# Late modulation in bursts of two k-tiles, and a smaller spacing of the recurrence's level pairs, in a hybrid decoder step

## Chip, cores and metric

The kernel runs on one core of one Trainium2 chip. The metric is the device time of one execution in microseconds (us); the span is the time from the first to the last instruction of the profiled execution.

## The reference

One decoder layer is applied to a prompt of 512 tokens and to 8 x 4 sample tokens with a cached past; both lie side by side as 544 token columns. All of it is fp32.

- A conditioning vector per sequence (9 in all) gives six modulation vectors: `mod = silu(c) @ w_ada + b_ada`, split into `sh1, sc1, g1, sh2, sc2, g2`.
- `h = rmsnorm(x) * (1 + sc1) + sh1`, and `proj = h @ w_in` is split into the queries, keys and values of an attention (8 heads of 64), the inputs of a gated linear recurrence (4 heads of 128) and two gates.
- The attention is block-sparse; for the sample tokens it reads 2048 cached rows per sequence through a page table.
- The recurrence is `S_t = diag(f_t) S_{t-1} + k_t v_t^T, o_t = S_t^T q_t`, followed by an rmsnorm over its 128 features and a gate.
- `mixed = sigmoid(ga) * (o_a @ w_a) + sigmoid(gb) * (o_b @ w_b)`, `x += g1 * (mixed @ w_o)`.
- A second modulated rmsnorm with `sc2, sh2`, a gated feed-forward with a causal convolution (`w_up`, `w_down`), `x += g2 * ...`, and a final rmsnorm.

`g1`, `sh2`, `sc2` and `g2` are not needed before `w_o`; they are the late modulation.

## The kernel before

Features stand on the 128 partitions, tokens along the free axis, in two halves of 272 columns. Every large product `W @ X` is made of three matmuls in fp32r (high part by high part, high by low, low by high). A weight chunk of four 128 x 128 tiles is loaded by SP's queue (`weights`, L206), rounded by ScalarE (`whi`), subtracted by VectorE (`wlo`), and used for twelve matmuls on each half of the tokens. So half a chunk, twelve matmuls, is the unit in which the main work advances (`pieces`, L296).

The order of TensorE's instructions is the order in which the program writes them, from the pool of the projections to `finish_sides` in L1262 (a manual schedule for TensorE alone; the other engines' order is made by the framework). It is set by a planner in the kernel itself. `Paced` (L101) keeps a clock of its own: each matmul adds `(0.006 + n * ns) * cols / 128` us, with n moving columns and ns 0.00044 for fp32r and 0.00167 for fp32, and 0.095 us are added when the shape of the array tile changes. The main work is a generator, `run_jobs` (L1125), which takes projection jobs in the order `ORDER` and then the products with `w_a` (`last_jobs`, L1252). Beside it run side generators; each yields how many us from now it is due again, and whether its next step is tiled, which means that it works on 32 columns of the array. After each half chunk `weave` calls `serve` (L273):

```
            if flat:
                run(flat[0])
            elif due and (len(due) > 1 or pe.t - due[0].due > due[0].slack or pe.mode[1] < 128):
                run(due[0])
```

A step that is not tiled runs when it is due. A tiled step runs when another is due too, when it is over `SLACK` = 2.5 late, or when the array is in a narrow mode already. The tiled sides here are these:

- `moba` (L708), the cached attention: 16 sets of scores and 16 of values, one every `SETS` = 7.2.
- `recur` (L1037), the recurrence on the prompt: per head four pairs of levels (64 and 32, 16 and 8, 4 and 2, 1 and 0), each pair a burst of 32-column matmuls (`level_mm`), then `yield LV, True`. After a head's last pair, `rec_gather` makes `rec_out` due 6.5 later, and the next head's decay work makes `rec_turn` due 8.0 after its first pair was prepared; both are full-width.
- `ada_late` (L1150), the late modulation, calls `ada_rest` (L1074) for two slabs of `w_ada`. Each has eight k-tiles of 128 x 2048 (1 MB). The tile `wadl` has two buffers, and its loads are issued by ScalarE's queue. The four quarters of the array each take 512 columns of a k-tile with the 32 padded conditioning columns `cs`; they accumulate in one PSUM bank over the eight k-tiles. The slab's result is copied into another buffer of the same tag, transposed and added to the bias.

`recur_sample` (L1164) is the recurrence on the sample tokens, two heads at a time; it starts a pair of heads when their `ob` is there, and has two tiled steps in it (the state products `QEs`), due 6.0 and 5.0 after the step before. It ends with the norm: for each head a square on ScalarE and a matmul with a matrix of 1/128. `ada_late` and `recur_sample` become sides when both attentions are done and the job then running is finished. After the main work, `finish_sides` runs what is left. Then the recurrence's output is scaled, split into `obh` and `obl`, and multiplied by `w_b`, then `w_o`, `w_up`, `w_down`.

Of the kernel before, what the change touches and what calls it, by code (L numbers as in the profile page):

```python
# [9 lines left out]
F32 = mybir.dt.float32  # L10
# [38 lines left out]
LNEXP = "natural_log_exp_and_others"  # L49
NPG = 9  # L50
WR, WS = 4, 3
SLACK, LT, SETS, LV, ADA = 2.5, 3.0, 7.2, 7.0, 3.6
ORDER = "k0 v0 k1 k2 k3 v1 v2 v3 f0 q0 i0 f1 q1 i1 f2 q2 i2 f3 q3 i3 a0 a1 a2 a3 a4 a5 a6 a7 g0 g1 g2 g3"
LATE = ("a4", "a5", "a6", "a7")
LAST = "b0 b1 b2 b3 b4 b5 b6 b7"
# [83 lines left out]
def layer_kernel(ctx, tc, i, o):  # L139
    nc = tc.nc  # L140
    sync, act, dve, pool, pe = nc.sync, nc.scalar, nc.vector, nc.gpsimd, Paced(nc.tensor)
# [11 lines left out]
    def gbank():  # L153
        return bank("g", NG)
# [10 lines left out]
    def mbank():  # L165
        return bank("macc", 1)
# [30 lines left out]
    def tt(out, a, b, op):  # L197
        return dve.tensor_tensor(out, a, b, op=op)  # L198
# [140 lines left out]
    cs = pC.tile([128, 8, 32], F32, name="cs")  # L339
# [733 lines left out]

    def ada_rest(sl, v0):  # L1074
        pa = mbank()
        for k in range(8):
            w = pT_.tile([128, 4, 512], F32, name="wadl", tag="wadl", bufs=2)
            act.dma_start(w, i["w_adl"][sl, k])
            yield ADA, True
            for g in range(4):  # L1080
                pe.matmul(pa[32 * g:32 * g + 32, :], cs[:, k, :], w[:, g, :], start=k == 0, stop=k == 7,
                          skip_group_check=True)
        sm = pT_.tile([128, 512], F32, name="smr", tag="wadl", bufs=2)
        dve.tensor_copy(sm, pa)
        yield 4.0
        pt = gbank()
        for c in range(4):
            pe.transpose(pt[:, 128 * c:128 * c + 128], sm[:, 128 * c:128 * c + 128], ident)
        pv = pt.rearrange("p (c g r) -> p c g r", c=4, g=4)
        for c in range(4):  # L1090
            for v in range(2):
                tt(modT[:, v0 + v, slice(c, 8, 4), :], pv[:, c, 2 * v:2 * v + 2, :9],
                   bada[:, v0 + v, slice(c, 8, 4), None].to_broadcast([128, 2, 9]), OP.add)
# [45 lines left out]
    pT_ = tc.alloc_tile_pool(name="rec", bufs=1, reuse_waits="tile")  # L1139
# [10 lines left out]
    def ada_late():  # L1150
        yield from ada_rest(0, 2)
        yield from ada_rest(1, 4)
        dve.scalar_tensor_tensor(modT[:, 4], modT[:, 4], 1.0, n2g[:, :, None].to_broadcast([128, 8, 9]),
                                 op0=OP.add, op1=OP.mult)
# [378 lines left out]
```

## Time and profile before

| | us |
|---|---|
| median of 3 runs | 979.36 |
| lowest and highest run | 977.35, 980.24 |
| profiled execution, its time | 979.07 |
| its span | 977.4 |
| TensorE busy in the span | 945.6 |

The profiled execution is 0.29 us below the median. A row of the timeline gives start and duration in us from the span's start; matmuls are pipelined, so a duration is longer than the distance to the next start. An fp32 matmul of the program shows as two records, so one modulation k-tile is eight records. In the stretches, the clock is the granted share of TensorE's full speed.

### The profile page before, as it was taken

How to read it: one execution, taken by the hardware profiler on the slowest of the kernel's cores; microseconds unless marked ns; L12 is line 12 of the kernel's file. 1: busy time of each engine (PE TensorE's matmuls, PEld its weight loads, DVE VectorE, ACT ScalarE, POOL GpSimd, SP SyncE). 2: the span in 40 equal slices, each digit the busy share in tenths (PEclk: the TensorE clock that was granted, in tenths of full speed). 3: DMA queues.
4: the chain of work that ended last, by engine and by line, in shares of the span. 5: the costliest groups of instructions: out<-in, count | busy, mean ns of one | idle time of the engine just before them, and what ended most of it. 6: DMA issues, size and time to landing. Idle time of an engine off the chain costs nothing.

```text
span 977.4 us, 23999 instructions
## 1 busy us (share of the span) xinstructions
PE 945.6 (97%) x8951; PEld 870.8 (89%) x8951; DVE 579.4 (59%) x1488; ACT 471.7 (48%) x942; POOL 103.1 (11%) x164
## 2 busy tenths in 40 slices
PE   5999999999999999999999999999999999999994
PEld 3898888877779988889998999999999999999994
DVE  5654546454657868755886676655555555555553
ACT  4344645543554645232544466544444444555452
POOL 1221222212210000000042200000000000001011
PEclk9999999999999999999999999999999999999997
DMA  9799999989695465473246143222222223566661
GB/s 361 283 363 374 360 332 341 332 289 340 237 358 186 165 209 183 161 276 119 65 147 212 45 130 126 99 90 87 87 87 88 87 90 92 175 178 188 196 175 67
DMA packets 89430, 190.06 MB, mean 194 GB/s; under 512 B 10337, under 2 KB 17634, under 8 KB 87266
## 3 DMA queue, kind: packets, MB, share of 16 engines
q1 hardware_dynamic: 75826, 140.74, 42.5%
q0 software_dynamic: 8160, 26.75, 7.6%
q10 hardware_dynamic: 5328, 21.05, 6.1%
q8 instruction: 70, 1.15, 0.5%
q14 instruction: 46, 0.38, 0.1%
HBM read 181.47 MB, written 7.02 MB: 193 GB/s over the span
## 4 chain that ended last, share of the span: by engine, by line
PE 74%; DVE 2%; ACT 1%; issue 1%; DMA 1%; POOL 0%; DVEq 0%; ACTq 0%; POOLq 0%
PE g L123 64%; PE macc L123 4%; PE s L123 2%; PE acc L123 1%; DMA wraw<-in_w_o 1%; PE s L127 1%; DVE wlo L198 1%; PE g L127 0%; POOL tgb L1281 0%; DVE hl L1283 0%; PE ms L123 0%; DVE tgb L1279 0%; ACT hh L195 0%; DVE tga L1461 0%; DVE wol L198 0%
## 5 line engine op out<-in xcount | busy, mean ns | idle before, releaser
L198 DVE TENSOR_TENSOR wlo<-wraw,whi 128x512 fp32r<-128x512 f32 (+1 forms) x300 | 203.2, 679 | 208.3 <-ACT whi L195 204.3
L195 ACT ACTIVATE whi<-wraw 128x512 fp32r<-128x512 f32 (+1 forms) x300 | 185.5, 619 | 258.2 <-PE g L123 237.3
L123 PE MATMUL g<-hh,whi 128*128 128x272 f32 x712 | 212.2, 299 | 1.3 <-ACT hh L195 1.0
L123 PE MATMUL g<-hl,whi 128*128 128x272 f32 x712 | 205.4, 289 | 0.7 <-DVE hl L1283 0.7
L123 PE MATMUL g<-hh,wlo 128*128 128x272 f32 x712 | 205.4, 288 | 0.6 <-DVE wlo L477 0.5
L123 PE MATMUL g<-h2h,whi 128*128 128x272 f32 x704 | 202.3, 289 | 0.0
L123 PE MATMUL g<-h2l,whi 128*128 128x272 f32 x704 | 201.3, 287 | 0.0
L123 PE MATMUL g<-h2h,wlo 128*128 128x272 f32 x704 | 198.8, 288 | 0.0
L123 PEld LDWEIGHTS g<-hh,whi 128*128 128x128 f32 x712 | 134.1, 188 | 16.7 <-issue 11.8
L123 PEld LDWEIGHTS g<-hl,whi 128*128 128x128 f32 x712 | 134.3, 189 | 1.3 <-DVE hl L1283 0.9
L123 PEld LDWEIGHTS g<-hh,wlo 128*128 128x128 f32 x712 | 134.0, 188 | 1.0 <-DVE wlo L477 0.7
L123 PEld LDWEIGHTS g<-h2l,whi 128*128 128x128 f32 x704 | 132.4, 188 | 0.1
L123 PEld LDWEIGHTS g<-h2h,whi 128*128 128x128 f32 x704 | 132.3, 188 | 0.2
L123 PEld LDWEIGHTS g<-h2h,wlo 128*128 128x128 f32 x704 | 130.8, 188 | 0.0
L123 PE MATMUL g<-ah,wlo 128*128 128x272 f32 x352 | 101.3, 288 | 1.2 <-DVE wlo L198 1.2
L123 PE MATMUL g<-ah,whi 128*128 128x272 f32 x352 | 101.8, 289 | 0.0
L123 PE MATMUL g<-al,whi 128*128 128x272 f32 x352 | 101.5, 288 | 0.0
L123 PEld LDWEIGHTS g<-ah,wlo 128*128 128x128 f32 x352 | 66.1, 188 | 1.5 <-DVE wlo L198 1.4
L123 PEld LDWEIGHTS g<-ah,whi 128*128 128x128 f32 x352 | 66.3, 188 | 0.1
L123 PEld LDWEIGHTS g<-al,whi 128*128 128x128 f32 x352 | 66.2, 188 | 0.1
L1323 POOL TENSOR_TENSOR sq<-sq,sq 128x272 f32<-128x272 f32 x24 | 20.9, 872 | 385.9 <-ACT sq L1314 374.1
L1417 DVE SCALAR_TENSOR_TENSOR cv<-U,sv,cv 128x560 f32<-128x560 f32 x44 | 35.3, 802 | 16.5 <-ACT cv L1415 15.7
(313 smaller groups left out, 1480.5 us busy)
## 6 DMA issues: line engine op xcount, KB each, us to landing
wraw<-in_w_up SPq DMA_DIRECT2D x98, 256.0 KB, 2.5
wraw<-in_w_in SPq DMA_DIRECT2D x82, 256.0 KB, 4.5
wraw<-in_w_down SPq DMA_DIRECT2D x80, 256.0 KB, 2.9
pg<-in_K SPq DMA_DIRECT2D x77, 256.0 KB, 6.7
pg<-in_V SPq DMA_DIRECT2D x77, 256.0 KB, 6.8
wadl<-in_w_adl ACTq DMA_DIRECT2D x16, 1024.0 KB, 5.8
pg<-in_K POOLq DMA_DIRECT2D x51, 256.0 KB, 6.0
pg<-in_V POOLq DMA_DIRECT2D x51, 256.0 KB, 6.2
```

What stands on the lines that cost most here:

```text
L123: return self.eng.matmul(out, lhsT, rhs, **kw)
L127: return self.eng.transpose(out, in_, ident)
L195: return act.activation(out, in_, AF.Copy, scale=scale)
L198: return dve.tensor_tensor(out, a, b, op=op)
L1323: pool.tensor_tensor(sqa[f], sqa[f], s, op=OP.add)
L1417: dve.scalar_tensor_tensor(a, U[:, t:t + W], cw[:, t, j:j + 1], a, op0=OP.mult, op1=OP.add)
```

## The change

The late modulation takes two k-tiles at a time: both loads are issued, 7.2 us later both are due, and their eight matmuls are issued together. Before, it was one load, 3.6 us, four matmuls. The number of buffers of `wadl` stays at two. `LV`, the time after which the recurrence's next pair of levels is due, goes from 7.0 to 6.0.

```diff
-SLACK, LT, SETS, LV, ADA = 2.5, 3.0, 7.2, 7.0, 3.6
+SLACK, LT, SETS, LV, ADA = 2.5, 3.0, 7.2, 6.0, 3.6
...
     def ada_rest(sl, v0):
         pa = mbank()
-        for k in range(8):
-            w = pT_.tile([128, 4, 512], F32, name="wadl", tag="wadl", bufs=2)
-            act.dma_start(w, i["w_adl"][sl, k])
-            yield ADA, True
-            for g in range(4):
-                pe.matmul(pa[32 * g:32 * g + 32, :], cs[:, k, :], w[:, g, :], start=k == 0, stop=k == 7,
-                          skip_group_check=True)
+        for k0 in range(0, 8, 2):
+            ws = [pT_.tile([128, 4, 512], F32, name="wadl", tag="wadl", bufs=2) for _ in range(2)]
+            for w, k in zip(ws, (k0, k0 + 1)):
+                act.dma_start(w, i["w_adl"][sl, k])
+            yield 7.2, True
+            for w, k in zip(ws, (k0, k0 + 1)):
+                for g in range(4):
+                    pe.matmul(pa[32 * g:32 * g + 32, :], cs[:, k, :], w[:, g, :], start=k == 0, stop=k == 7,
+                              skip_group_check=True)
         sm = pT_.tile([128, 512], F32, name="smr", tag="wadl", bufs=2)
```

## Rows read from the trace of the kernel before

**Rows 1.** The page, busy time, share of the span and instructions of each engine.

```profile
PE 945.6 (97%) x8951; PEld 870.8 (89%) x8951; DVE 579.4 (59%) x1488; ACT 471.7 (48%) x942; POOL 103.1 (11%) x164
```

**Rows 2.** Stretches: length, busy us (instructions) of each engine, clock, DMA share, GB/s.

```profile
480.00:488.00 8.00, 7.57 (x56) 6.95 (x56) 6.72 (x14) 2.47 (x4) 0.52 (x1) 1.00 0.25 66
517.00:521.50 4.50, 2.74 (x16) 1.92 (x15) 2.82 (x13) 3.16 (x6) 0.12 (x1) 1.00 0.48 176
521.50:525.50 4.00, 3.79 (x18) 3.74 (x18) 3.64 (x8) 2.32 (x5) 1.93 (x2) 0.57 0.44 146
```

**Rows 3.** TensorE's timeline around one burst: start, duration, what ran.

```profile
321.56 0.29 PE L123 MATMUL g<-hl,whi 128*128 128x272 f32 x1
321.69 0.29 PE L123 MATMUL g<-hh,wlo 128*128 128x272 f32 x1
321.91 1.07 PE L123 MATMUL macc<-wadl,cs 128*32 128x512 f32 x8
322.79 0.78 PE L123 MATMUL s<-EX 128*32 128x32 f32 x64
323.50 0.39 PE L123 MATMUL g<-hh,whi 128*128 128x272 f32 x1
323.73 0.29 PE L123 MATMUL g<-hl,whi 128*128 128x272 f32 x1
```

**Rows 4.** TensorE's timeline, three other bursts with modulation matmuls.

```profile
329.71 1.07 PE L123 MATMUL macc<-wadl,cs 128*32 128x512 f32 x8
...
345.43 1.06 PE L123 MATMUL macc<-wadl,cs 128*32 128x512 f32 x8
...
429.97 1.06 PE L123 MATMUL macc<-wadl,cs 128*32 128x512 f32 x8
```

**Rows 5.** The tile wadl: its matmuls (ns min/median/max, first and last start), time to landing.

```profile
L123 PE MATMUL macc<-wadl,cs x128: 592/593/618, 321.9 to 441.2; 128*32 128x512 f32 x128
...
DMA to landing us min/median/max: 4.7/5.8/8.9
```

**Rows 6.** TensorE's timeline in the cached attention: sets (macc), pairs of levels (EX).

```profile
282.62 0.76 PE L123 MATMUL s<-EX 128*32 128x32 f32 x64
...
291.27 1.92 PE L123 MATMUL macc<-pg,pT 128*32 128x512 f32 x16
...
299.98 1.92 PE L123 MATMUL macc<-pg,pT 128*32 128x512 f32 x16
...
302.57 0.51 PE L123 MATMUL s<-EX 128*32 128x32 f32 x33
```

**Rows 7.** TensorE's timeline at the end of the recurrence.

```profile
413.27 0.48 PE L123 MATMUL s<-EX 128*32 128x32 f32 x32
...
420.66 0.61 PE L123 MATMUL acc<-hs,V 128*128 128x128 f32 x4
...
434.17 0.62 PE L123 MATMUL acc<-s,QEs 128*32 128x512 f32 x2
...
441.60 1.03 PE L123 MATMUL acc<-s,QEs 128*32 128x512 f32 x4
...
454.12 0.63 PE L123 MATMUL s<-rv,kvx 96*128 96x512 f32 x2
...
471.38 1.08 PE L123 MATMUL s<-EX,con 128*128 128x272 f32 x4
...
482.64 0.39 PE L123 MATMUL g<-obh,whi 128*128 128x272 f32 x1 [0.40 <-ACT obh L195]
```

**Rows 8.** VectorE's timeline between the norm matmuls and the splits.

```profile
473.66 0.43 DVE L1242 TENSOR_SCALAR rr<-s 128x272 f32<-128x272 f32 x1
...
483.82 1.37 DVE L198 TENSOR_TENSOR obl<-ob,obh 128x544 fp32r<-128x544 f32 x2
```

**Rows 9.** ScalarE's timeline between the norm matmuls and the splits.

```profile
474.18 1.12 ACT L1246 ACTIVATE rr<-rr 128x1088 f32<-128x1088 f32 x1 [1.73 <-issue]
...
475.93 1.10 ACT L1248 ACTIVATE rr<-rr 128x1088 f32<-128x1088 f32 x1
```

## The prediction

> **What bounds the kernel now.** I read the page's engine table first: TensorE is busy for 945.6 of 977.4 us [rows 1], so between the start and the last stage only two things can change the time: what TensorE has to do, and whether it is ever left without work. The changed lines act between about 280 and 480 us. I therefore read TensorE's timeline there, burst by burst, and then the join at 481 us, where the last `w_a` matmul is followed by the first `w_b` matmul, which needs the normalised recurrence output.
>
> A burst in which the array works on quarters of 32 columns looks like [rows 3]: full-width matmuls start at 321.56 and 321.69 (0.125 apart, before rounding), the burst at 321.91, a modulation k-tile takes 0.88, a pair of levels 0.71, and after it the second full-width matmul comes 0.23 after the first. So going in costs 0.22 - 0.125 = 0.095 us and coming out about 0.1: some 0.2 per burst.
>
> The join has no slack. The last of the four norm matmuls of the recurrence starts at 471.38 [rows 7]; from it a chain of VectorE and ScalarE work leads to the split `obh`/`obl`, whose last piece is written from 483.82 on for 1.37 us (two instructions) [rows 8], and TensorE waits 0.40 us for `obh` at 482.64 [rows 7]. In the 8 us around it TensorE is idle for 8.00 - 7.57 = 0.43 us [rows 2]. So an earlier recurrence gains at most about 0.4 us here; a later one is paid for almost in full. When the recurrence ends is set by the planner, so the change has to be followed through it.
>
> **The change, part by part.**
> *Work on TensorE.* Nothing is added or removed: 128 records of modulation matmuls before [rows 5], eight for each of 16 k-tiles, and the same after. What may go is mode switches. Of the 16 k-tiles only two stand in a burst with no other narrow work beside them, at 345.43 and 429.97 [rows 4]; the others share their burst with a pair of levels or with another 32-column step. Two bursts less are 2 x 0.2 = **-0.4 us**.
> The Trainium skill, TensorEngine Tiling (Array Packing), Key Properties, says that a change of tiling mode drains TensorE; read alone, 16 bursts made into 8 would spare 8 such round trips. By that the sum would be 8 x 0.2 = -1.6 us instead of -0.4.
>
> *The pace.* The planner's clock, from the code: half a chunk (12 matmuls) 1.508, a k-tile 0.861, a pair of levels 0.345 to 0.505, a switch 0.095. Tiled steps run when two are due, or when one is 2.5 late.
> Before: a burst at T with the k-tile first makes it due again at T+4.56 and the pair at T+8.43. The planner looks at T+3.04, 4.54, 6.05, 7.56. At 7.56 the k-tile is over 2.5 late and goes, and at its end the pair is due too. Period 7.56; measured 329.71 - 321.91 = 7.80 [rows 3, 4], so a burst takes 0.24 more than planned.
> After: pair at T, then two k-tiles. The pair is due at T+6.57, the modulation at T+9.49. At 8.42 the pair alone is 1.85 late, which is allowed; at 9.93 both are due. **Period 9.93 instead of 7.56**: the single k-tiles had been what carried the pairs along, and `LV` of 6 in place of 7 does not make up for it. Without a partner a pair goes after 9.71 (11.2 with 7).
>
> *The start.* `LV` also acts during the cached attention. The pair of 282.62 [rows 6] is then due 1.0 earlier, 289.2, and the attention set of 291.27 [rows 6] was due by 289.75 at the latest (it became due after the pair at 282.6 and comes every 7.2). So both are probably due one half chunk earlier, and by the same arithmetic the last set (299.98) and the pair of 302.57 [rows 6] come 1.5 to 3 earlier, and the second loop starts one job (four half chunks) earlier. Carried on through the code's rules, the pairs then stand, after against before by the planner's clock: second head 310.9 (313.0), 318.6 (322.7), 326.7 (330.3), 336.7 (337.8); third 347.1 (349.0), 356.7 (358.2), 365.3 (366.3), 373.4 (373.8); fourth 384.0 (383.2), 393.5 (392.7), 401.8 (401.3), 412.1 (409.5). The lead of 2 us is used up, and the last pair, at 413.27 in the trace [rows 7], is 2.6 late.
>
> *The end of the recurrence.* Output of head 3 (420.66 [rows 7]): planner 419.4 against 416.7, +2.7. Before, leftover k-tiles come due beside the sample steps and pull them forward; after, all are done by about 400, and the two state products of 434.17 and 441.60 [rows 7] have to be 2.5 late before they go: +3.7 and +5.0. The last state update (454.12 [rows 7]): 455.0 against 448.8, **+6.3**. From there on nothing changes, so the last norm matmul stands at 471.38 + 6.3 = 477.7.
>
> *What that costs.* From the norm matmul to the end of the last split it took 485.2 - 471.4 = 13.8 before, much of it because VectorE also had the `w_a` evictions. The chain alone: four norm matmuls 1.08 [rows 7], two evictions 0.43 each, a logarithm 1.12 and an exponential 1.10 [rows 8, 9], then on VectorE products and split at 0.7 each, 4 to 5 of them: 7.5. I take 9, near the lower end, as only some evictions are left: 486.7. `w_a` ends at about 481.3 - 0.4 = 480.9; six matmuls of the first two k-tiles fill 0.75. New idle 486.7 - 480.9 - 0.75 = 5.0, less the 0.4 of before: **+4.6 us** (bounds: 0 if the recurrence isn't late, +10 if it is 9 late and the chain takes 11).
> *Clock.* After a stretch of 4.5 us in which TensorE was idle for 1.8, its granted clock is 0.57 over 4 us [rows 2] (for most of them its 1.2 GHz level): 4 x 0.43 = 1.7 us of lost work. A gap of 5 us is longer, so I take **+1.7** (bounds 0 and 2 x 1.7).
> *The new wait.* Both buffers are now filled together, and only when both k-tiles of the burst before are computed. One load lands in 4.7 to 8.9 us, median 5.8 [rows 5]. The loads go out about 2.6 after the burst began and the second k-tile is wanted about 11.7 after it: 9.1 us, just over the longest landing. One or two late issues: **+0.5** (bounds 0 and 7 bursts x 2 = 14; nearer to 0, as 8.9 is still inside). Behind a waiting TensorE stand the `g` matmuls of the running chunk; on ScalarE's queue the weight copies stand behind the load that waits for the burst, but the burst is done when it is issued. SP's weight loads share the DMA engines with 2 MB at once; four raw buffers are 12 us of cover, so 0.
>
> Sum: -0.4 + 4.6 + 1.7 + 0.5 = +6.4. The profiled execution took 979.07 (span 977.4); the median of the runs is 979.36, 0.3 above. I say 985.0, rounding down since the start may gain another half chunk.
>
> **Rivals.**
> *Not late.* Every step of the planner is one half chunk, 1.5 us. If two or three fall the other way (the head start in the attention part is 3 to 4.5 us and holds), the last norm matmul stays at or before 472; that is the point from which it decides. Then only switches and the 0.43 us of the join are left: -0.4 - 0.4 = 978.3, no change. For it: LV is smaller everywhere, and the pairs start earlier; against: the period of 9.93, which the same arithmetic that gave 7.56 (7.80 measured) gives with room on both sides. If besides that what the Trainium skill says of drains (TensorEngine Tiling (Array Packing), Key Properties) showed in all 8 bursts, it would be 977.1.
> *Loads late.* ScalarE issues a load late behind its other work, both k-tiles wait in most of 7 bursts, 1 to 1.5 us each, on top of the tail: 985 + 5 = 990. For it: the room of 0.2 us above; against: 8.9 is the longest of 16, and the first of the two k-tiles needs its load only as fast as now.
> *Planner step without head start.* The set of 291.27 stays where it is: all of the rest 2 to 3 us later, 988.
>
> **How the numbers follow.** About 0.3%, 2.9 us, is what a measurement of this kernel can tell from no change: 976.4 to 982.3 counts as the same. Late tail as worked out: 0.50, its own range 981.5 to 988. Not late: 0.28, of which 0.08 is faster by over 0.3% (with stalls further on shortened as well) and the rest the same. Loads late 0.10, no head start 0.12: both slower. Of the main case 0.07 ends within 0.3%. So faster 0.08, same 0.20 + 0.07 = 0.27, slower 0.43 + 0.22 = 0.65. The range 977.5 to 990 takes in both signs and leaves out the ends.
>
> **What would show it.** Right: bursts some 10 us apart with 16 modulation records each; a last pair of levels near 415, the last norm matmul near 478; a wait of TensorE for `obh` or `obl` of 3 to 7 us at about 481 and a granted clock near half behind it; no wait for `wadl`. Wrong: the last norm matmul at or before 472 and no gap at the join (not late); waits for `wadl` of over 5 us in sum (loads late); or a chain so short without the evictions that a late norm costs nothing.

## The result, and the profile after

The changed kernel took 985.49 us (median of 4 runs, 984.34 to 986.49) against 978.36 us for the kernel before beside it. The ratio is 1.0066, 95% interval 1.0049 to 1.0083: slower by 4.8 to 8.1 us. The profiled execution took 986.49 us with a span of 984.8.

The page's engine row of the changed kernel answers to [rows 1]:

```profile
PE 949.4 (96%) x8951; PEld 874.4 (89%) x8951; DVE 580.2 (59%) x1488; ACT 472.9 (48%) x942; POOL 102.9 (10%) x164
```

TensorE has the same 8951 instructions. Of its 3.8 us more, part has nothing to do with the change. From 22.5 to 27 us, among instructions that are the same in both kernels, TensorE ran at full clock in the profile of the kernel before and at half clock in that of the changed one. The stretch in the kernel before and, below it, in the changed one (length, busy us of PE, PEld, DVE, ACT, POOL, clock, DMA share, GB/s):

```profile
22.50:27.00 4.50, 4.50 (x58) 3.96 (x58) 2.49 (x8) 0.00 (x0) 0.75 (x2) 1.00 1.02 411
```

```profile
22.50:27.00 4.50, 4.50 (x42) 3.40 (x42) 0.69 (x2) 0.00 (x0) 0.00 (x0) 0.50 1.01 407
```

The pair of levels of 282.62 [rows 6], up to which nothing has moved, stands later in TensorE's timeline of the changed kernel:

```profile
284.79 0.76 PE L123 MATMUL s<-EX 128*32 128x32 f32 x64
```

Every difference below has these 284.79 - 282.62 = 2.17 us taken off (in the other profiles what the same pair shows, -0.8 to +3.1). The end then is 5.26 us later than before.

TensorE's timeline of the changed kernel, the rows that answer to [rows 7]:

```profile
419.18 0.48 PE L123 MATMUL s<-EX 128*32 128x32 f32 x32
...
427.02 0.61 PE L123 MATMUL acc<-hs,V 128*128 128x128 f32 x4
...
441.13 1.05 PE L123 MATMUL acc<-s,QEs 128*32 128x512 f32 x4
...
449.85 1.05 PE L123 MATMUL acc<-s,QEs 128*32 128x512 f32 x4
...
463.46 0.63 PE L123 MATMUL s<-rv,kvx 96*128 96x512 f32 x2
...
480.69 1.08 PE L123 MATMUL s<-EX,con 128*128 128x272 f32 x4
```

With 2.17 taken off, the last pair of levels is 3.7 late, the output of head 3 4.2, the state products 4.8 and 6.1, the last state update 7.2, the last norm matmul 7.1 (480.69 - 2.17 - 471.38).

TensorE's timeline at the join of `w_a` and `w_b` in the changed kernel, start, duration, and in brackets the idle time before it and what ended it:

```profile
484.50 0.29 PE L123 MATMUL g<-oah,wlo 128*128 128x272 f32 x1
486.93 0.65 PE L123 MATMUL g<-obh,whi 128*128 128x272 f32 x3 [2.14 <-ACT obh L195]
488.66 0.60 PE L123 MATMUL g<-obl,whi 128*128 128x272 f32 x1 [1.08 <-DVE obl L198]
489.05 0.43 PE L123 MATMUL g<-obh,wlo 128*128 128x272 f32 x1
...
494.90 0.30 PE L123 MATMUL g<-obl,whi 128*128 128x272 f32 x1
```

Two waits, 3.2 us where there was one of 0.40, and behind them matmuls of 0.43 us where 0.29 is usual. The stretches of the changed kernel, written as above, the last two of them what 517 to 525.5 was in [rows 2]:

```profile
485.00:488.50 3.50, 0.65 (x3) 0.43 (x3) 3.50 (x7) 2.43 (x4) 0.00 (x0) 0.93 0.45 114
488.50:494.80 6.30, 6.14 (x27) 6.15 (x28) 3.54 (x6) 1.32 (x2) 0.00 (x0) 0.50 0.05 20
...
526.00:530.50 4.50, 2.74 (x18) 2.08 (x17) 2.99 (x14) 3.41 (x6) 0.66 (x1) 1.00 0.54 175
530.50:534.50 4.00, 4.00 (x34) 4.00 (x34) 3.79 (x7) 2.27 (x6) 1.39 (x2) 1.00 0.57 177
```

For 6.3 us the granted clock is 0.50 (1.2 GHz), which costs 3.15. But the stretch in the `w_o` stage that had 0.57 before [rows 2] has 1.00 now, although TensorE is busy for the same 2.74 us ahead of it: 4 x 0.43 = 1.7 us come back.

VectorE's and ScalarE's timelines of the changed kernel between the norm and the split, answering to [rows 8, 9]:

```profile
482.97 0.43 DVE L1244 TENSOR_SCALAR rr<-s 128x272 f32<-128x272 f32 x1
...
486.61 1.35 DVE L198 TENSOR_TENSOR ob<-ob,rr 128x544 f32<-128x544 f32 x2
487.88 1.35 DVE L198 TENSOR_TENSOR obl<-ob,obh 128x544 fp32r<-128x544 f32 x2
...
490.66 1.42 DVE L198 TENSOR_TENSOR obl<-ob,obh 128x544 fp32r<-128x544 f32 x2
```

```profile
483.49 1.12 ACT L1248 ACTIVATE rr<-rr 128x1088 f32<-128x1088 f32 x1 [1.73 <-issue]
...
485.24 1.09 ACT L1250 ACTIVATE rr<-rr 128x1088 f32<-128x1088 f32 x1
486.24 1.20 ACT L195 ACTIVATE obh<-ob 128x544 fp32r<-128x544 f32 x2
```

There are two pairs of splits, first that of heads 0 and 1 and then that of heads 2 and 3. Both waits at the join are for the first pair. It is behind the last norm matmul all the same: the two engines have the exponential of heads 2 and 3 (485.24) and their product with it (486.61) ahead of it in their order. The first pair ends 489.23 - 480.69 = 8.5 us after the last norm matmul, the second, for which TensorE does not wait, 492.08 - 480.69 = 11.4 us after it. In the kernel before, where the second ended 13.8 us after the last norm matmul, the end of the first stands in VectorE's timeline, 480.27 - 471.38 = 8.9 us after it, ahead of the end of `w_a`:

```profile
478.91 1.36 DVE L198 TENSOR_TENSOR obl<-ob,obh 128x544 fp32r<-128x544 f32 x2
```

Ahead of the join, TensorE's timeline of the changed kernel shows a burst of two k-tiles and three short waits, of which the kernel before had none between 265 us and the join:

```profile
299.44 0.40 PE L123 MATMUL g<-hh,whi 128*128 128x272 f32 x1 [0.24 <-ACT tga L1099]
...
330.00 1.92 PE L123 MATMUL macc<-wadl,cs 128*32 128x512 f32 x16
...
353.13 1.06 PE L123 MATMUL macc<-wadl,cs 128*32 128x512 f32 x8 [0.46 <-DMA wadl<-in_w_adl]
...
372.28 0.39 PE L123 MATMUL g<-hh,whi 128*128 128x272 f32 x1 [0.68 <-DVE G L842]
```

So the account of the trace is: waits ahead of the join 1.4, at the join 3.2 - 0.4 = 2.8, half clock at the join +3.15, half clock in the `w_o` stage -1.7, a wait of 0.2 there less: 5.4 to 5.5, against 5.26.

### The profile page after: what moved, and what is told of

It is laid out like the page before. It is cut to its first block, busy times and chain, and to the rows that moved or that the text cites. A ratio compares the mean times of both kernels' runs of the same rounds, so it can differ in the third digit from the quotient of the medians.

```text
span 984.8 us, 23994 instructions
## 1 busy us (share of the span) xinstructions
PE 949.4 (96%) x8951; PEld 874.4 (89%) x8951; DVE 580.2 (59%) x1488; ACT 472.9 (48%) x942; POOL 102.9 (10%) x164
## 4 chain that ended last, share of the span: by engine, by line
PE 69%; DVE 3%; DMA 3%; ACT 2%; issue 1%; POOL 0%; DVEq 0%; SPq 0%; ACTq 0%; POOLq 0%
PE g L123 60%; PE macc L123 4%; PE s L123 2%; PE acc L123 1%; DVE wlo L198 1%; DMA wadl<-in_w_adl 1%; DMA pg<-in_V 1%; DMA wraw<-in_w_o 1%; PE s L127 1%; DMA wraw<-in_w_up 0%; PE g L127 0%; POOL tgb L1283 0%; DVE hl L1285 0%; DVE tgb L1281 0%; ACT whi L195 0%
```

## The experiments

All twelve kernels are read in the same way. Counted in the order of TensorE's instructions, "room" is the number of matmuls of the main work (0.125 us each) between the last norm matmul and the end of the products with `w_a`. "Ahead" and "join" are TensorE's waits from 265 us to the join and at it; "clock" is the half clock's cost, length x (1 - clock) from 480 to 510 and from 510 to 540 (to about 0.3). "Sum" is all that less the 2.2 of the kernel before, "trace" the end against the kernel before. The ratio is that of the medians' comparison, with its interval.

| kernel | room | ahead | join | clock | sum | trace | ratio (95%) |
|---|---|---|---|---|---|---|---|
| before | 72 | 0 | 0.4 | 0 + 1.8 | 0 | 0 | 1 |
| after | 24 | 1.4 | 3.2 | 3.3 + 0 | 5.7 | 5.3 | 1.0066 (1.0049 to 1.0083) |
| bursts only | 0 | 3.0 | 7.1 | 5.1 + 1.8 | 14.8 | 13.5 | 1.0144 (1.0127 to 1.0161) |
| LV only | 48 | 1.3 | 1.6 | 0 + 1.8 | 2.5 | 3.8 | 1.0035 (1.0021 to 1.0048) |
| eager sample | 24 | 3.0 | 3.2 | 3.3 + 0 | 7.3 | 7.1 | 1.0117 (1.0100 to 1.0133) |
| filler (24 matmuls, 3.0) | 24 | 1.6 | 0.4 | 0 + 1.8 | 4.6 | 4.2 | 1.0051 (1.0033 to 1.0069) |
| late norm | 12 | 0 | 2.8 | 3.3 + 0 | 3.9 | 3.5 | 1.0039 (1.0025 to 1.0053) |
| eager second pair | 60 | 2.1 | 0.8 | 0 + 0 | 0.7 | 0.9 | 1.0016 (1.0006 to 1.0026) |
| half loads | 24 | 1.0 | 3.2 | 3.3 + 0 | 5.3 | 4.6 | 1.0050 (1.0036 to 1.0065) |
| half loads, due 6.0 | 36 | 2.6 | 1.9 | 1.8 + 1.8 | 5.9 | 7.4 | 1.0063 (1.0046 to 1.0079) |
| LV 5.0, due 9.6 | 120 | 4.3 | 0 | 0 + 1.8 | 3.9 | 3.2 | 1.0033 (1.0024 to 1.0042) |
| LV 5.0 | 72 | 0.3 | 0.4 | 0 + 0 | -1.5 | -0.9 | 1.0009 (0.9997 to 1.0022) |

In "bursts only", 1.6 of the 3.0 are waits among the norm matmuls behind the end of `w_a`, and its last 0.6 of 1.8 of half clock lie at 510 to 540, 1.2 behind them. Sum and trace differ by up to 1.5 us. The sum has no term for switches of the array (LV only has 26 narrow bursts, on 32 columns, from 282 us on, the kernel before 23) and none for waits in the `w_o` stage (half loads with a due time of 6.0 have one of 0.94 us there). The profile of the eager sample is that of its fastest run, 2.8 us under its median, so that its trace shows less than its ratio. The kernel with the filler in `w_o` and its combination with the row "LV 5.0, due 9.6" are told below.

**Theory**: the change makes the recurrence's norm late by letting level pairs and k-tiles wait for each other longer, and this is paid at the join. **Rivals**: the loads; the smaller `LV` as a cost or a remedy of its own; the bursts themselves.

**1. Bursts alone, 2. LV alone.** The two parts of the change apart:

```diff
-SLACK, LT, SETS, LV, ADA = 2.5, 3.0, 7.2, 6.0, 3.6
+SLACK, LT, SETS, LV, ADA = 2.5, 3.0, 7.2, 7.0, 3.6
```

in the changed kernel (bursts alone), and the same line the other way round in the kernel before (LV alone).

> The change without its smaller spacing: LV back at 7.0, the bursts of two k-tiles kept. Theory (the burst of two slows the level pairs from 7.56 to 9.93 by the planner, the recurrence ends late, the join at w_b pays): the spacing within bursts stays 9.93, the head start is gone, so the last norm matmul comes as late as with the change or 1 to 4 us later, and the time is 985 to 989. Rival (the smaller LV does the harm, by crowding the planner): back to 978 to 980.

> The change without its bursts: LV 6.0, single k-tiles as before. Theory: a burst at T still makes the k-tile over 2.5 late at T+7.56 and the pair is due then (7.43), so the period stays 7.56, the last norm matmul stays within 2 us of 471.4 and the time is 976.5 to 979.5, no change. Rival (LV does the harm): 984 or more. Rival (LV is what brings a gain that the bursts spoil): under 975.5.

Bursts alone: 993.53 us (992.14 to 994.95), the way the theory has it, but more than its 985 to 989. TensorE's timeline shows the norm itself behind the end of `w_a` and two long waits after it:

```profile
486.61 1.16 PE L123 MATMUL s<-EX,con 128*128 128x272 f32 x4 [0.17 <-DVE rr L1244]
...
493.27 1.05 PE L123 MATMUL g<-obh,whi 128*128 128x272 f32 x3 [5.51 <-ACT obh L195]
495.87 0.60 PE L123 MATMUL g<-obl,whi 128*128 128x272 f32 x1 [1.56 <-DVE obl L198]
```

LV alone: 982.73 us (981.15 to 985.95), between the two forecasts and a miss. Read from the timelines, the bursts are, by start in whole us (start offset taken off; P a pair of levels, W modulation k-tiles, Q state products of the sample tokens):

```
before      314P 322PW 330PW 338PW 345W 350PW 359PW 367PW 375PW 386PW 394PWQ 403PWQ 412PW 422W 430W 434WQ 441WQ
after       313P 322P 328PW 338PW 349PW 359PW 369P 376PW 389PW 399PQ 402W 407PQ 415PW 439Q 448Q
bursts only 314P 325PW 335PW 345PW 356PW 368P 375PW 385PW 398W 400P 408Q 409PW 418PQ 430P 453Q 461Q
LV only     313P 322PW 330PW 338PW 346W 349P 354W 360PW 368PW 376PW 386PW 394PW 399Q 403PW 408WQ 416PW 423W 429W 436WQ 446Q
due 6.0     313P 322P 328PW 336PW 345W 349P 357PW 371P 376PW 385W 390P 396PWQ 406PWQ 418P 439Q 448Q
LV 5.0      308P 318PW 326P 330W 335P 342W 346P 353PW 364P 370PW 382PW 392PQ 396W 401PQ 407W 411P 433Q 442Q
```

With bursts alone the distance is 10.2 (325, 335, 345), the 9.93 of the forecast and a burst's extra, where the kernel before has 7.8. With LV alone the distance stays at about 8, yet the pair comes due ahead of its k-tile (349P, 354W) and a state product finds no partner (399Q); the last pair is then 2.6 late and its state products 2.8 and 4.6. So a smaller LV is neither harmless nor a cost by itself: it moves which steps meet. Together with the bursts it takes 8 us off them (993.53 against 985.49).

**3. The sample steps no longer wait for a partner.** In the changed kernel:

```diff
-            yield 6.0, True
+            yield 6.0
...
-                yield 5.0, g == 0
+                yield 5.0
```

> The changed kernel, with the two state products of the sample recurrence run as soon as they are due (6.0 and 5.0), not held until another narrow step is due or 2.5 us have passed. Nothing else moves. Theory (the late recurrence is what costs): planner 430.5 and 437.2 instead of 433.5 and 441.7, so the last norm matmul comes 4.5 us earlier, the gap at w_b shrinks by 3 to 4 us with the slow clock behind it, and the time is 979.5 to 982.5. Rival (the loads of two k-tiles cost the time): 985, no change, or up to 0.4 more for switches.

990.06 us (987.23 to 991.07): the wrong direction. Its TensorE timeline:

```profile
399.15 1.05 PE L123 MATMUL acc<-s,QEs 128*32 128x512 f32 x4
...
406.04 1.05 PE L123 MATMUL acc<-s,QEs 128*32 128x512 f32 x4
...
415.05 0.47 PE L123 MATMUL s<-rv,kvx 96*128 96x512 f32 x1 [2.06 <-DVE s L1220]
```

The state products of the first two heads came when due, but in the changed kernel they had carried two level pairs with them (399PQ, 407PQ). Alone, they left the last pair 10.1 us late instead of 3.7 (423.4 and 417.0 against 413.3), and the state update waited 2.06 for VectorE. A step that costs nothing by being late had been what let another run in time. The join is as in the changed kernel (room 24, the same two waits), so the waits ahead of it (3.0 for 1.4) are most of the 1.8 us by which the trace is longer than that of the changed kernel. By the ratios it is 5 us; what the slower runs add is not shown.

**4. A filler at the join.** Ahead of the products with `w_b`, in the changed kernel, 24 matmuls that nobody reads:

```diff
     finish_sides(su, al_, rec)
+    fb = gbank()
+    for _ in range(24):
+        pe.matmul(fb[:, :HALF], oah[:, 0, 0:128], oah[:, 0, half(0)], start=True, stop=True)
```

> The changed kernel with 24 matmuls that nobody reads (0.125 us each, 3.0 us) put between the last w_a and the first w_b matmul, where TensorE waits 2.1 and 1.1 us. Theory (half of the join's cost is the clock: it is at 0.50 for 6.3 us after the gap): the clock stays at 1.00, the first w_b matmuls wait as long as before, and the time falls by 2.5 to 3.2 us to 982 to 983. Rival (the gap itself is all, or the w_o stage takes it back): no change, or slower by up to 1 us where the filling outlasts the wait.

983.86 us (982.17 to 986.24), between the two forecasts. The stretches behind the join and in the `w_o` stage of this kernel:

```profile
485.00:495.00 10.00, 9.43 (x69) 8.66 (x68) 8.93 (x16) 4.30 (x7) 0.95 (x1) 1.00 0.18 51
529.00:533.00 4.00, 4.00 (x27) 4.00 (x26) 3.14 (x7) 1.81 (x4) 0.91 (x2) 0.76 0.67 198
```

The join's half clock is gone, and the one of the `w_o` stage is back. So what the clock costs here is the difference of the two, about 1.5; the kernel gained 1.1 by the trace and 1.5 by the ratios.

**5. Only the norm late.** In the kernel before, with bursts and pace untouched:

```diff
-        yield 4.0
+        yield 12.0
         po = abank()
```

> The kernel before the change, with one number altered: the pause of the sample recurrence ahead of its last products is 12.0 instead of 4.0 by the planner's clock, so that the norm alone comes some 8 us later and nothing else moves. Theory (the join pays for a late norm): the last norm matmul is 7 to 8 us late, about as with the change, and the time rises by 3.5 to 6 us, to 982.5 to 985. Rival (the chain after the norm has slack, and the change costs elsewhere): within 1.5 us of before.

982.76 us (982.46 to 984.30), a hit. The last norm matmul is 7.6 late, about as in the changed kernel (7.1), nothing waits ahead of the join, and TensorE's timeline at the join and the `w_o` stretch read:

```profile
483.67 0.65 PE L123 MATMUL g<-obh,whi 128*128 128x272 f32 x3 [2.16 <-ACT obh L195]
484.90 0.60 PE L123 MATMUL g<-obl,whi 128*128 128x272 f32 x1 [0.59 <-DVE obl L198]
```

```profile
526.00:530.00 4.00, 3.79 (x28) 3.57 (x29) 3.85 (x7) 2.71 (x6) 2.06 (x2) 1.00 0.36 126
```

The wait for `obh` is that of the changed kernel to 0.02 us, and the `w_o` stage runs at 1.00 here too. A late norm alone costs 3.5 us by the trace and 3.8 by the ratio, of 5.3 and 6.5 that the change costs.

**6. Only the second pair of heads doesn't wait.** The edit of run 3 for heads 2 and 3 alone, whose state products had no pair left to carry:

```diff
-            yield 6.0, True
+            yield 6.0, p == 0
...
-                yield 5.0, g == 0
+                yield 5.0, g + p == 0
```

> The changed kernel, with the two state products run as soon as they are due for heads 2 and 3 alone, where no pair of levels is left to be carried by them (for heads 0 and 1 they stay as they are: run early there, they left the last three pairs without a partner, 6 us later). Theory: the last norm matmul comes 4 to 5 us earlier than with the change (some 2.5 late against before, start loss taken off), and the time falls to 981 to 983. Rival (lateness of the norm isn't what costs): 985 to 986.

981.15 us (978.60 to 982.59), a hit: by the ratios 4.9 of 6.5 us are back (0.5% of 979). Its TensorE timeline has 0.82 us at the join and, ahead of it, a longer wait for a load:

```profile
354.54 1.07 PE L123 MATMUL macc<-wadl,cs 128*32 128x512 f32 x8 [1.39 <-DMA wadl<-in_w_adl]
...
488.54 0.75 PE L123 MATMUL g<-obh,whi 128*128 128x272 f32 x3 [0.82 <-ACT obh L195]
```

**7. Half loads, 8. half loads and an earlier due time.** In the changed kernel, four buffers of half the size, so that no load waits for a burst (half of the late modulation's weights are left out); in run 8 also `yield 6.0, True`:

```diff
-            ws = [pT_.tile([128, 4, 512], F32, name="wadl", tag="wadl", bufs=2) for _ in range(2)]
+            ws = [pT_.tile([128, 2, 512], F32, name="wadl", tag="wadl", bufs=4) for _ in range(2)]
...
-                act.dma_start(w, i["w_adl"][sl, k])
+                act.dma_start(w, i["w_adl"][sl, k][:, :2])
...
-                    pe.matmul(pa[32 * g:32 * g + 32, :], cs[:, k, :], w[:, g, :], start=k == 0, stop=k == 7,
+                    pe.matmul(pa[32 * g:32 * g + 32, :], cs[:, k, :], w[:, g % 2, :], start=k == 0, stop=k == 7,
```

> The changed kernel with loads of half the size (two of the four column groups of a k-tile, used twice; so half of the late modulation's weights are left out and its values are not the reference's) in four buffers of half the size. The matmuls and their order stay. Theory: only the wait for a load goes (0.46 us shown, 1.0 from start to start), the time is 983.5 to 985.5. Rival (the loads of 2 MB at once are the main cost, by their own wait or by delaying the weights): 978 to 981.

> As the kernel with half loads (half of the weights of the late modulation left out), and the burst is due again after 6.0 in place of 7.2. Theory: both are then due at the planner's look at 8.42, not 9.93, so bursts come 8.7 us apart in the trace instead of 10.2, the last pair of levels comes 4 to 10 us earlier than with the change, the last norm matmul at or before that of before, and the time is 976.5 to 980. Rival (the number of matmuls in a burst, not its due time, sets the spacing): 984 or more.

Run 7: 984.67 us (980.85 to 984.73), a hit: the waits for `wadl` are gone, and by the trace 0.7 us with them. Run 8: 985.95 us (983.60 to 989.12), a miss: an earlier due time did not bring the pairs closer. The list above shows why: the k-tiles now come due ahead of the pairs and go without them (345W, 385W), the pairs go alone (349P, 371P, 390P), and the slab's end meets work of VectorE. TensorE's timeline of that place:

```profile
368.27 0.66 PE L127 MATMUL g<-con,smr 128*128 128x128 f32 x4 [1.14 <-DVE vi L854]
...
370.13 0.63 PE L127 MATMUL g<-con,viT 128*128 128x128 f32 x4 [1.20 <-DVE modT L198]
```

**9. to 11. Room at the join by two numbers, a filler in the `w_o` stage, and both.** Run 9 is the changed kernel with these two edits; run 10 is the kernel before with the filler (the last diff); run 11 has both.

```diff
-SLACK, LT, SETS, LV, ADA = 2.5, 3.0, 7.2, 6.0, 3.6
+SLACK, LT, SETS, LV, ADA = 2.5, 3.0, 7.2, 5.0, 3.6
...
-            yield 7.2, True
+            yield 9.6, True
```

```diff
+            if w == "w_o" and m == 3 and c == 0 and halves == (0,):
+                fb = gbank()
+                for _ in range(11):
+                    pe.matmul(fb[:, :HALF], hh[:, 0, 0:128], hh[:, 0, half(0)], start=True, stop=True)
```

> The changed kernel with two numbers moved: the next pair of levels due after 5.0 instead of 6.0, two k-tiles due after 9.6 instead of 7.2. The order of TensorE's instructions, counted from the programs, has this many main matmuls (0.125 us each) between the last norm matmul and the end of the products with w_a: 72 in the kernel before, 24 in the changed one, 0 in the one with bursts alone, 48 with LV alone, 60 with the second pair of heads not waiting; 120 here. Theory (the late norm is what the change pays for): with 120 the last norm matmul stands about 15 us ahead of the join, TensorE waits for no obh or obl there, the clock stays at 1.00 from 450 to 505, the loads have 2.4 us more than in the changed kernel and none is waited for; with two narrow bursts fewer than before (19 against 21) the median is 977.5 to 980. Rival (bursts of two k-tiles cost by themselves, by stalls ahead of the join as in the runs with LV alone or with the k-tiles due after 6.0, 2 to 3 us there): 981 to 983.5, with the w_a products ending 2 to 3 us later than before.

> The kernel before, with 11 matmuls of 272 columns added whose result nobody reads, in the products with w_o ahead of the half chunk for which TensorE waited 1.44 us at 521 (11 x 0.125 = 1.38 us). In the kernel before that gap is followed by half clock, (1 - 0.57) x 4 = 1.7 to 1.8 us; in the changed kernel and with the late norm alone, which had their half clock at the join with w_b, the same gap is followed by none. Theory (the w_o stage gave back its own half clock, which is why 2 us of the join's loss came back): with the gap filled the clock stays at 1.00 from 510 to 540 and the kernel is 1.2 to 1.8 us faster, 977.3 to 978. Rival (the clock falls elsewhere afterwards, or the 1.8 us come back at another wait for weights): within 0.5 us of the kernel before.

> The two edits of the two runs before it together: level pairs due after 5.0, k-tiles in twos after 9.6, and the 11 unread matmuls in the w_o stage. If both theories hold the parts add up: no wait at the join (-0.4), two bursts fewer (-0.4), no half clock at w_o (-1.2 to -1.8): 976 to 977.5, faster than both kernels. If the bursts cost by themselves: 979.5 to 982.

Run 9: 982.70 us (981.33 to 984.08). The join has no wait, as the theory has it, and the kernel is still slower, as the rival has it. The time is lost ahead of the join; TensorE's timeline, and VectorE's for the middle one:

```profile
361.83 0.38 PE L127 MATMUL s<-con,K2s 128*32 128x128 f32 x2 [0.76 <-DVE kvx L198]
...
367.53 0.40 PE L123 MATMUL g<-hh,whi 128*128 128x272 f32 x1 [2.31 <-DVE G L842]
...
379.03 0.68 PE L123 MATMUL acc<-hs,V 128*128 128x128 f32 x4 [1.22 <-DVE hs L1019]
```

```profile
363.12 2.33 DVE L198 TENSOR_TENSOR rv<-kvx,con 96x1024 fp32r<-96x1024 f32 x2
...
367.04 0.44 DVE L842 SCALAR_TENSOR_TENSOR G<-th,g 128x272 f32<-128x272 f32 x1
```

The earlier pairs bring the first sample heads forward, and their 2.33 us on VectorE (`rv`) now stand in the same stretch as the next head's preparation, ahead of an eviction (`G`) without which TensorE's next half chunk has no bank.

Run 10: 979.68 us (976.88 to 981.00), ratio 0.9996, 0.9984 to 1.0008. TensorE's timeline and the stretch behind the gap:

```profile
521.88 1.54 PE L123 MATMUL g<-hh 128*128 128x272 f32 x11
523.47 0.39 PE L123 MATMUL g<-hh,woh 128*128 128x272 f32 x1
```

```profile
523.50:528.00 4.50, 4.29 (x32) 4.07 (x33) 4.32 (x8) 2.75 (x6) 2.06 (x2) 1.00 0.45 123
```

In the profiled execution the clock stays at 1.00 and the end comes 1.4 us earlier; over the runs no gain shows. The interval just reaches 1.6 us, so this is inconclusive; perhaps the clock doesn't fall there in most executions, which no run shows. Run 11: 982.56 us (980.20 to 984.18), ratio 1.0025 (1.0015 to 1.0035); the waits of run 9 are there again (5.2 us ahead of the join), and the sum that was hoped for isn't.

**12. LV of 5.0 and nothing else.** The changed kernel with the first of run 9's two edits.

> The changed kernel with one number moved: the next pair of levels is due after 5.0 instead of 6.0 (7.0 was the run with bursts alone). Counted from the programs, 72 main matmuls stand between the last norm matmul and the end of the products with w_a, as many as in the kernel before (changed kernel 24); the pairs of heads 1 and 2 stand up to 6 us of main work earlier than before. Theory (two prices: a late norm is paid at the join with w_b, steps brought forward are paid in waits for VectorE ahead of it): no more than about 0.4 us of waiting at the join, no half clock there, but 1 to 2.5 us of waits for VectorE or loads before 481, as in the run with 5.0 and 9.6 (4.3 us): 980 to 982. Rival (the norm alone decides): no waits before the join, 978.5 to 979.7. A second rival (bursts of two cost whatever their pace): 983 or more.

978.29 us (977.38 to 982.30) beside 978.22 for the kernel before: no difference. That is just under the first rival's 978.5 to 979.7, and not the 980 to 982 of the theory with two prices. TensorE's timeline, and its stretch that answers to the first of [rows 2]:

```profile
471.61 1.08 PE L123 MATMUL s<-EX,con 128*128 128x272 f32 x4
...
482.88 0.77 PE L123 MATMUL g<-obh,whi 128*128 128x272 f32 x2 [0.40 <-ACT obh L195]
```

```profile
480.00:488.00 8.00, 7.57 (x56) 6.95 (x56) 6.72 (x14) 2.47 (x4) 0.28 (x1) 1.00 0.23 66
```

The norm matmul and the join are those of the kernel before [rows 2, 7], and 0.30 us is all that TensorE waits ahead of it. So bursts of two k-tiles need not cost anything: at this pace the ratio leaves between -0.3 and +2.2 us for them. With due time 7.2 and `LV` at 7.0, 6.0 and 5.0 the same bursts took 993.53, 985.49 and 978.29 us. The pairs are not closer together at 5.0 than at 6.0 (103 us from the first to the last of heads 1 to 3, against 104); they start at 308 instead of 313. What 5.0 gives is the head start that the slower pace uses up.

None of the twelve is faster than the kernel before by more than its interval.

## Why the prediction was right

The forecast was 985.0, the median 985.49, and the case it rested on is the one that came: the recurrence ends late, the norm with it, and the join pays. Run 5 shows that a late norm alone does this, run 6 that most of the loss goes when the norm comes earlier.

That the number came within 0.5 us is in part luck. The forecast added +6.4 to 979.36 and rounded that down by 0.8. The trace, with the loss at its start taken off, is 5.26 longer, and the medians differ by 7.1 (978.36 was the kernel before beside it). The sum -0.4 + 4.6 + 1.7 + 0.5 came as +2.8 at the join, +1.4 from the clock and +1.4 from waits ahead of the join: one term too large, one too small, one right by two errors. Point by point:

- **The pace.** Forecast a period of 9.93, about 10.2 with a burst's extra; the runs show 10.2 with bursts alone. In the changed kernel it comes only here and there. The twelve pairs of heads 1 to 3 are 9.5 apart on average there (104.0 / 11) against 9.0 (99.3 / 11), close to what the forecast had when it carried the pairs through. That LV of 6.0 would not make up for the bursts holds, though it made up for 8 of 15 us.
- **The start.** The set of 291.27 came 1.5 earlier, as forecast. The rest of that step failed: the last set and the pair of 302.57 came 1.0 earlier, not 1.5 to 3, and the second loop did not begin a job earlier. The first pair of head 1 stood at 313.0 for 314.0, so the head start was 1.0 us where the forecast had 2.1. With LV of 5.0 it is 5.7.
- **The end of the recurrence.** Forecast +2.6, +2.7, +3.7, +5.0, +6.3, +6.3; measured +3.7, +4.2, +4.8, +6.1, +7.2, +7.1. About 1 us on each is what TensorE waited ahead of them (the waits of 0.24, 0.46 and 0.68), which a planner's clock doesn't know: with the end of `w_a`, 1.1 later too, taken off, the norm is 6.0 late, which is the 48 matmuls of room that are lost.
- **The join.** This step has the right place and a wrong wait. The forecast let the six matmuls of heads 0 and 1 run and then waited for the last split, 9 us after the norm. The last split took 11.4, and TensorE did not wait for it: it waited for the split of heads 0 and 1, which the forecast took as ready. That this ended 8.5 after the norm, so that TensorE went on at 488.66 - 2.17 = 486.5 for a forecast of 486.7, is luck. The idle time is smaller than the forecast (+2.8 for +4.6) mostly because `w_a` ended 1.1 later than before instead of 0.4 earlier: those waits stand ahead of the join. Nor was a later recurrence paid for almost in full: 6.0 us of lost room became 2.8 us of waiting, in part as the first split had been ready 1.1 us before the first `w_b` matmul (481.34).
- **The clock.** Forecast +1.7, net +1.4, but that is luck, as the step was wrong in its working: the join alone cost 3.15, since the half clock lasted 6.3 us and not 4, and the stretch that I priced it from [rows 2] ran at 1.00. Nothing in the forecast said that one loss can take the place of another.
- **The new wait.** One late load, 0.46, for a forecast of 0.5; run 7 prices all loads at 0.7 by the trace. The forecast's own sign (no wait for `wadl`) had it at none. Not foreseen: 0.68 us for an eviction on VectorE and 0.24 for one on ScalarE.
- **Switches.** From the pair of 282.62 on, TensorE's timeline has 21 narrow bursts for 23, two less as forecast, so 0.4 us by [rows 3]; no run measures it by itself. The Trainium skill, TensorEngine Tiling (Array Packing), Key Properties, says that a change of tiling mode drains TensorE. Read alone, with eight bursts less, that would be 1.6 us, but the trace has only two bursts fewer. Most k-tiles had shared their burst with other narrow work before, which pays for a switch in any case.

The rivals: "not late" fell here (the last norm matmul at 478.5, with the deciding point at 472), but LV of 5.0 is that case, at its price (978.3). "Loads late" fell with 0.46 and 0.7 us. "No head start" was half true (1.0 of 2.1 us), but the time was not its 988.

What stays open: whether the clock falls at 521 us in most executions of the kernel before, how much of the difference of the medians is the half clock at 22.5 us, and why the same idle time is followed by half clock in one kernel and not in another.

## What to carry to other kernels

Where steps wait for a partner to share a mode, a due time is not a rate: a change to one of them decides which steps meet, and the cost appears where the last of them feeds the main work. Count in the instruction order how much main work lies between the side work's end and its use, and hold it against the chain in between, here 8.5 to 8.9 us, some 70 matmuls. Room of 120, 72, 60, 48, 36, 24, 12 and 0 matmuls went with waits of 0, 0.4, 0.8, 1.6, 1.9, 3.2, 2.8 and 7.1 us, and this can be counted before anything runs. The waits ahead of the join have to be read from VectorE's timeline. Look which part of a chain the main work asks for first; it need not be the last. And add half-clock stretches as a difference: filling one brought another back.

## What the runs showed of the hardware

A gap of 1.44 us at the end of a stretch with the same busy time (2.74 of 4.5 us) was followed by 4 us at a mean clock of 0.57 in the kernel before [rows 2] and by 1.00 in the changed one; with the late norm the same gap was followed by 1.00 too. In most of these kernels, a half-clock stretch at the join and one in the `w_o` stage excluded each other; with the eager second pair and with LV of 5.0 there was neither, with bursts alone and with half loads due after 6.0 there were both. After the two waits at the join of the changed kernel (3.2 us in sum) the half clock lasted 6.3 us of nearly full work. And from 22.5 to 27 us the same instructions ran at 0.50 in the profile of the changed kernel and at 1.00 in that of the kernel before; what follows stood 2.17 us later in the first.
